# Low parts of weights by accumulating transfers, pair sums in place, the residual through SP's queue

## The chip, the cores and the metric

The kernel runs on one core of a Trainium2 chip. The core has five engines with an instruction queue each: PE (matmul), DVE (vector), ACT (scalar, activations), POOL (GpSimd) and SP (issues transfers). They run beside each other and wait for each other by semaphores; each works through its own queue in order. SBUF is the on-chip memory, PSUM the banks into which PE writes. The metric is the device time of one execution in microseconds (us), lower is better; the median over runs is compared.

## The reference, cut to what matters

One layer on 512 prompt tokens and 32 sample tokens (T = 544), width 1024, FFN width 2816, in float32:

```python
x = x + 0.5 * swiglu(rms_norm(x, ffn1_norm), ffn1_gate, ffn1_up, ffn1_down)
z = rms_norm(x, mix_norm) @ w_in                     # 3584 columns: qa ka va qb fb ib gb
x = x + concat(attention(qa, ka, va), silu(gb) * norm(hgrn2(qb, fb, ib))) @ w_out
x = x + 0.5 * swiglu(rms_norm(x, ffn2_norm), ffn2_gate, ffn2_up, ffn2_down)
def swiglu(x, w_gate, w_up, w_down):
    return (silu(x @ w_gate) * (x @ w_up)) @ w_down
```

The attention is block sparse on the prompt and, on the sample tokens, reads keys and values of 8 sequences from a paged cache. hgrn2 is a gated linear recurrence.

## The kernel before

**Matmuls in two parts.** All activations lie transposed: 128 features on the partitions, 544 tokens along a row, in two halves of 272. A float32 product is made of three faster ones: each operand is split into a high part, rounded (`hi`, float32r), and a low part, the rest (`lo` = value - hi), and `products` issues hi x hi, hi x lo and lo x hi. Of a weight, ACT makes the high part (a cast, `whi<-raw`) and DVE the low part (a subtraction, `wlo<-raw,whi`).

**Weights.** `weight_jobs` lists them in the order of use. A tile of 128 output columns is loaded in two halves ("units") of 4 x 128 rows by SP's queue into a raw buffer (`w_load`), split into a pair whi, wlo (`w_split`, `split_unit`), and freed when PE is done with it (`free_w`), which pumps the next ones (`w_pump`). There are 4 raw buffers and 4 pairs, and at most AHEAD = 4 units are split ahead. In the FFNs further buffers come from the tiles `xh`, `xl` of the normalised input once that is no longer needed (`more_slots`).

**Stages.** FFN1 (about 0 to 400 us of the trace), the middle stage (to about 830) and FFN2 (to the end). In each FFN gate and up of the first NREG = 5 blocks of 128 columns are plain products ("plain blocks"). The other 17 blocks use a scheme of seven products in place of eight (`hidden_paired`, `paired_gemm`): gate and up halves are combined into sums (tiles `S0` to `S3`, in `w_split`), two on DVE and two on POOL, and the right side into differences (`right_factors`, tiles `xw`). `right_factors` is a side task that is stepped between matmuls while the plain blocks run, PACE = 0.8 us after one another; the paired blocks start when it is done. In the middle stage `project` makes the 28 tiles of w_in, between which attention and recurrence run as side tasks; the 8 tiles of w_out follow, which add to the residual `y`. The residual has been parked in DRAM (`xs`) and is loaded back by POOL's queue.

**Order.** A recording layer (`Order`) plans the program by a model of the engines: it gives every instruction a start time and then issues each engine's instructions sorted by those times. So a change of what an operation is modelled to cost, or of which engine does it, moves other instructions too, on all engines. Side tasks fill PE's time as they become ready.

**Names.** `kn`, `qh`, `ql`, `kt`, `y_qk`, `pT`, `sc` belong to the prompt's attention; `KV`, `PT` to the sample's (gathers by POOL from the cache); `rec`, `at`, `oS`, `y_h`, `hkt` to the recurrence; `ob`, `AS`, `attn` to the sample's attention output. In the order printed below numbers behind a name count buffers; `L284` and `L288` are one helper line that records every operation.

Of the kernel before, what the change touches and what calls it, by code (L numbers as in the profile page):

```python
# [30 lines left out]
FGROUPS = ((0, 8), (8, 8), (16, 6))  # L31
# [22 lines left out]
PACE = 0.8  # L54
# [124 lines left out]
class Engine:  # L179
# [74 lines left out]
class Order:  # L254
# [103 lines left out]
    def dma(self, part, size, names, cost=0.06):  # L358
        s = self.fit(part, self.start(part, names), cost)
        e = self.fit("dma", s + cost + 1.5, size / 330e3) + size / 330e3  # L360
# [51 lines left out]

class Build:
# [34 lines left out]

    def weight_jobs(self):
# [7 lines left out]
        def plain(m, nk, r0, c0):  # L457
            out.append({"paired": False, "src": quarters(m, nk, r0, c0), "nk": nk // 2, "raw": [], "done": 0})

        def ffn(p):  # L460
            gate, up, down = (a[p + n][0] for n in ("_gate", "_up", "_down"))
            for g0, ng in FGROUPS:
                for f in range(g0, g0 + ng):
                    if f < NREG:
                        plain(gate, KD, 0, 128 * f)
                        plain(up, KD, 0, 128 * f)
                    else:
                        out.append({"paired": True, "nk": KD // 2, "raw": [], "done": 0,
                                    "src": quarters(gate, KD, 0, 128 * f) + quarters(up, KD, 0, 128 * f)})
                for m in range(KD):  # L470
                    plain(down, ng, g0, 128 * m)

        ffn("ffn1")
        for n, j in IN_ORDER:
            plain(a["w_in"][0], KD, 0, COLS[n] + 128 * j)
        for m in range(KD):
            plain(a["w_out"][0], KD, 0, 128 * m)
        ffn("ffn2")
        return out

    def room(self, kind, job):

        free = [x for x in self.slots[kind] if x["used"] < x["bufs"] and (x["extra"] is None or job["paired"])]
# [13 lines left out]
    def more_slots(self, pool):  # L497

        for i in range(KD):
            if i < 2:  # L500
                for t in ("xh", "xl"):
                    self.slots["raw"].append({"pool": pool, "tags": (f"{t}{i}",), "bufs": 1, "used": 0, "freed": [],
                                              "extra": pool})
            else:
                self.slots["w"].append({"pool": pool, "tags": (f"xh{i}", f"xl{i}"), "bufs": 1, "used": 0,
                                        "freed": [], "extra": pool})
# [9 lines left out]
    def w_load(self):  # L516
# [7 lines left out]
        self.nc.sync.dma_start(raw[:, :job["nk"]], job["src"][len(job["raw"])])  # L524
# [5 lines left out]
    def split_unit(self, src, nk, x):  # L530
        nc = self.nc
        hi, lo = self.take_slot(x, (F32R, F32R))
        nc.scalar.copy(hi[:, :nk], src[:, :nk])
        nc.vector.tensor_tensor(lo[:, :nk], src[:, :nk], hi[:, :nk].bitcast(F32), op=ALU.subtract)
        return hi, lo, x

    def w_split(self):
# [4 lines left out]
        if len(job["raw"]) <= (3 if job["paired"] else n):  # L542
            return False
        x = self.room("w", job)
        if x is None:
            return False
        nk = job["nk"]
        if job["paired"]:
            (a11, a12, a21, a22) = (r for r, _ in job["raw"])
            if n == 0:  # L550
                S = [self.tl(self.sums, [128, 4, 128], f"S{i}") for i in range(4)]
                for i, (e, p, q, op) in enumerate(((self.nc.vector, a21, a22, ALU.add),
                                                   (self.nc.vector, S[0], a11, ALU.subtract),
                                                   (self.nc.gpsimd, a11, a21, ALU.subtract),
                                                   (self.nc.gpsimd, a12, S[1], ALU.subtract))):
                    e.tensor_tensor(S[i][:, :nk], p[:, :nk], q[:, :nk], op=op)
                job["units"] = (a11, S[1], S[0], a12, S[2], S[3], a22)
            src = job["units"][n]
            self.units.append(self.split_unit(src, nk, x))
            drop = {0: (0, 2), 3: (1,), 6: (3,)}.get(n, ())  # L560
        else:
            self.units.append(self.split_unit(job["raw"][n][0], nk, x))
# [9 lines left out]
    def w_pump(self):  # L572
        while (len(self.units) < AHEAD and self.w_split()) or self.w_load():
# [69 lines left out]
    PAIRED = ((0, 0, True), (1, 4, True), (2, 3, True), (0, 1, False), (1, 5, False), (2, 2, False), (1, 6, False))  # L643

    def paired_gemm(self, xw, nk, evacs):
# [6 lines left out]
        for (b, r, first), evac in zip(self.PAIRED, evacs):  # L652
            w, = self.next_w(1)
            for k in range(nk):
                xh, xl = xw[k]
                self.products(ps[b], w, k, xh[:, r], xl[:, r], first and k == 0, k == nk - 1, not first)
# [4 lines left out]
    def right_factors(self, pool, x, gain):  # L661


# [4 lines left out]

        def lows(hi, lo, r, src):
            nc.scalar.copy(hi[:, r], src)  # L670
            nc.vector.tensor_tensor(lo[:, r], src, hi[:, r].bitcast(F32), op=ALU.subtract)

        def diff(out, p, q):
            nc.vector.tensor_tensor(out, p, q, op=ALU.subtract)

        for k in range(n):

            home, th, tl = self.hidden_home
# [1166 lines left out]
```

## Time and profile before

| | |
|---|---|
| median of 3 runs | 1205.38 us (1205.19 to 1206.52) |
| the profiled execution | 1210.65 us, its span 1208.9 us |
| mean granted clock of PE | 0.99 |
| DMA traffic | 144.74 MB, mean 120 GB/s |
| q1, transfers issued by SP and ACT | 106.60 MB, 30.6% of 16 engines' time |
| q0, transfers issued by POOL | 36.32 MB, 9.1% |

The profile is of one execution, and its times are counted from the span's start. PE's busy time says little alone, since matmuls overlap: a matmul of 272 columns is shown with some 0.29 us, but the next one starts 0.125 us later. The pace, the idle time and its releaser ("<-DVE kn" behind a row: PE had waited for DVE's write of kn) tell more. The granted clock falls to half for some microseconds around stretches in which PE stands still.

### The profile page before, as it was taken

What the parts mean: (1) busy time and instruction counts of PE and PEld (TensorE: products, weight loads), DVE (VectorE), ACT (ScalarE), POOL (GpSimd) and SP (SyncE); (2) the same over time, 40 slices, a digit from 0 to 9 for tenths busy, and PEclk for the clock granted to TensorE, in tenths of its full rate; (3) what the DMA queues carried; (4) which work ended last, traced back from release to release, by engine and by line L of the source; (5) the groups of instructions that cost most, each with busy time, mean ns of one, the idle gap of its engine ahead of it and who ended that gap; (6) DMA issues with size and microseconds to landing.
All of it is one profiled execution on the core that took longest, in us unless ns stands there. A gap on an engine that the chain in (4) does not pass through costs nothing.

```text
span 1208.9 us, 26320 instructions
## 1 busy us (share of the span) xinstructions
PE 1178.1 (97%) x10571; PEld 1113.7 (92%) x10571; DVE 858.5 (71%) x1729; ACT 551.9 (46%) x1125; POOL 228.3 (19%) x211
## 2 busy tenths in 40 slices
PE   8999999999999999989999999899999999999998
PEld 8989999999999988878878867799999999999998
DVE  6988559954875698877776557667977488736843
ACT  6455246532654345554556433344554266524632
POOL 3012012200202401000332344220020023102200
PEclk9999999999999999989999999899999999999999
DMA  5244453333314642322565776352344323323222
GB/s 161 79 123 114 133 148 97 97 106 87 87 54 135 193 129 69 97 72 74 181 195 160 235 262 222 111 158 79 93 118 131 97 81 104 106 87 88 63 79 82
DMA packets 216238, 144.74 MB, mean 120 GB/s; under 512 B 12035, under 2 KB 204067, under 8 KB 216116
## 3 DMA queue, kind: packets, MB, share of 16 engines
q1 hardware_dynamic: 205588, 106.60, 30.6%
q0 software_dynamic: 10432, 36.32, 9.1%
q8 instruction: 83, 1.36, 0.5%
q14 instruction: 39, 0.32, 0.1%
q10 hardware_dynamic: 96, 0.14, 0.0%
HBM read 133.94 MB, written 11.83 MB: 121 GB/s over the span
## 4 chain that ended last, share of the span: by engine, by line
PE 77%; DVE 13%; ACT 3%; DMA 3%; issue 2%; SPq 1%; POOL 0%; DVEq 0%; ACTq 0%; POOLq 0%
PE mm L284 51%; PE sm L284 26%; DVE wlo L284 3%; DVE xl L284 2%; DVE xwl L284 1%; DMA raw<-ffn_down 1%; ACT xh L284 1%; DVE t_h L284 1%; SPq L284 1%; ACT whi L284 1%; DVE hl L284 1%; ACT sq L284 1%; DMA raw<-ffn_up 1%; DVE S L284 1%; DMA KV<-cache_v,idx 1%
## 5 line engine op out<-in xcount | busy, mean ns | idle before, releaser
L284 PE MATMUL mm<-xh,whi 128*128 128x272 f32 x1216 | 365.0, 300 | 1.0 <-DVE t_g L284 0.5
L284 PE MATMUL mm<-xl,whi 128*128 128x272 f32 x1216 | 352.4, 290 | 5.4 <-DVE xl L284 5.2
L284 PE MATMUL mm<-xh,wlo 128*128 128x272 f32 x1216 | 353.2, 290 | 1.1 <-DVE wlo L284 1.1
L284 ACT CAST whi<-raw 128x512 fp32r<-128x512 f32 (+1 forms) x230 | 138.7, 604 | 261.4 <-PE mm L284 192.3
L284 PEld LDWEIGHTS mm<-xh,whi 128*128 128x128 f32 x1216 | 231.5, 190 | 18.2 <-issue 15.7
L284 PEld LDWEIGHTS mm<-xl,whi 128*128 128x128 f32 x1216 | 231.3, 190 | 6.4 <-DVE xl L284 6.2
L284 PEld LDWEIGHTS mm<-xh,wlo 128*128 128x128 f32 x1216 | 231.0, 190 | 2.1 <-DVE wlo L284 2.1
L284 DVE TENSOR_TENSOR wlo<-raw,whi 128x512 fp32r<-128x512 f32 (+1 forms) x230 | 165.1, 727 | 81.0 <-ACT whi L284 77.4
L284 POOL TENSOR_TENSOR S<-raw,raw 128x512 f32<-128x512 f32 x18 | 30.4, 1691 | 380.9 <-DMA raw<-ffn_up 261.1
L284 PE MATMUL mm<-hh,whi 128*128 128x272 f32 x352 | 101.5, 288 | 0.3 <-DVE x L284 0.3
L284 PE MATMUL mm<-hh,wlo 128*128 128x272 f32 x352 | 101.1, 287 | 0.0
L284 PE MATMUL mm<-hl,whi 128*128 128x272 f32 x352 | 101.1, 287 | 0.0
L284 PE MATMUL mm<-xwh,xh 128*128 128x272 f32 x296 | 85.4, 288 | 1.3 <-DVE t_h L284 0.8
L284 PE MATMUL sm<-xwl,xh 128*128 128x272 f32 x296 | 85.3, 288 | 0.0
L284 PE MATMUL mm<-xwl,xh 128*128 128x272 f32 x296 | 85.3, 288 | 0.0
L284 PE MATMUL sm<-xwh,xh 128*128 128x272 f32 x296 | 85.2, 288 | 0.0
L284 PE MATMUL mm<-xwh,xl 128*128 128x272 f32 x296 | 85.2, 288 | 0.0
L284 PE MATMUL sm<-xwh,xl 128*128 128x272 f32 x296 | 85.2, 288 | 0.0
L284 DVE TENSOR_TENSOR xl<-S,xh 128x512 fp32r<-128x512 f32 x84 | 66.0, 796 | 4.1 <-ACT xh L284 3.7
L284 PEld LDWEIGHTS mm<-hh,whi 128*128 128x128 f32 x352 | 66.3, 188 | 0.7 <-ACT whi L284 0.5
L284 ACT CAST xh<-S 128x512 fp32r<-128x512 f32 x84 | 51.8, 620 | 32.7 <-DVE S L284 13.7
L284 PEld LDWEIGHTS mm<-hh,wlo 128*128 128x128 f32 x352 | 66.2, 188 | 0.0
(325 smaller groups left out, 2639.2 us busy)
## 6 DMA issues: line engine op xcount, KB each, us to landing
raw<-ffn_down SPq DMA_DIRECT2D x64, 256.0 KB
raw<-ffn_gate SPq DMA_DIRECT2D x56, 256.0 KB
raw<-ffn_up SPq DMA_DIRECT2D x56, 256.0 KB
raw<-w_in SPq DMA_DIRECT2D x56, 256.0 KB
raw<-ffn_down SPq DMA_DIRECT2D x32, 192.0 KB
xl<-ffn_gate SPq DMA_DIRECT2D x16, 256.0 KB
xh<-ffn_up SPq DMA_DIRECT2D x16, 256.0 KB
xl<-ffn_up SPq DMA_DIRECT2D x16, 256.0 KB
```

The source lines that it names most:

```text
L284: call(*map(real, args), **{k: real(v) for k, v in kw.items()})
```

## The change

1. The low part of every unit of w_in and w_out (56 and 16), and of the second unit of gate and up in the FFNs' plain blocks (18), is made without DVE: ACT writes -hi into wlo, and a transfer issued by POOL adds the raw weight to it (`transfer` in `split_unit`). The raw buffer is held until that transfer has landed. There are six whi, wlo pairs in place of four, and in the middle stage up to six units are split ahead (AHEAD_MIX).
2. A paired block's sums are made in place, with other signs: a21 + a22 by an accumulating transfer (POOL's queue), a11 - a21 becomes a11 + a21 on POOL, and two in-place sums on DVE. The tiles S0 to S3 are gone; the extra buffers are ten raw ones and three pairs (were four and six). The first unit needs one raw half loaded, not four. The last one's parts are made with the second's. Right factors follow these signs (`Factors`), two steps each 1.1 us.
3. The residual `y` is loaded through SP's queue.
4. Smaller: the first up product is read from PSUM without copies, the first projection runs its two halves of tokens interleaved, POOL's ring for transfer descriptors gets 8192 bytes of a partition, and the planner has costs for transfers issued by POOL. The code for a paired down product (`down_paired`, FGROUPS[True]) is there, but both FFNs are called without it.

```diff
-PACE = 0.8
+AHEAD_MIX = 6
+PACE = 1.1
...
             if op == "dma_start":
-                s = self.order.dma(self.part, 4 * args[1].shape[0] * self.free(args[1]), names)
+                pool = self.part == "pool"
+                s = self.order.dma(self.part, 4 * args[1].shape[0] * self.free(args[1]), names,
+                                   1.3 if pool else 0.06, 3.0 if "accum_op" in kw else 1.5)
...
+class Factors:
...
+    def first(self):
+        return self.one(0, 0) + [self.diff(0, 1, 0)] + self.one(1, 0)
+    def right(self):
+        nc = self.nc
+        return [lambda: nc.vector.scalar_tensor_tensor(self.raw(0), self.raw(3), -1.0, self.raw(0),
+                                                       op0=ALU.mult, op1=ALU.subtract),
+                lambda: nc.vector.tensor_tensor(self.raw(1), self.raw(1), self.raw(3), op=ALU.add)] + self.two(2, 0)
+    def left(self):
+        return self.two(4, 2) + [self.diff(2, 2, 0)] + self.one(6, 2)
...
+        def paired(kind, nk, a11, a12, a21, a22, transfer):
+            job(kind, [a11, a21, a21 if transfer else None, a22, a12], nk)
+            out[-1]["transfer"] = transfer
...
         raw, = self.take_slot(x, (F32,))
-        self.nc.sync.dma_start(raw[:, :job["nk"]], job["src"][len(job["raw"])])
+        raw_k = raw[:, :job["nk"]]
+        i = len(job["raw"])
+        if job["paired"]:
+            parts = [r[:, :job["nk"]] for r, _ in job["raw"]]
+        if job["src"][i] is None:
+            self.nc.gpsimd.tensor_tensor(raw_k, parts[0], parts[1], op=ALU.add)
+        else:
+            self.nc.sync.dma_start(raw_k, job["src"][i])
...
+        if job["paired"] and i == 3:
+            self.nc.gpsimd.dma_start(parts[1], raw_k, accum_op=ALU.add)
...
-    def split_unit(self, src, nk, x):
+    def split_unit(self, src, nk, x, transfer=False):
+
         nc = self.nc
         hi, lo = self.take_slot(x, (F32R, F32R))
         nc.scalar.copy(hi[:, :nk], src[:, :nk])
+        if transfer:
+            nc.scalar.activation(lo[:, :nk], src[:, :nk], AF.Identity, scale=-1.0)
+            nc.gpsimd.dma_start(lo[:, :nk], src[:, :nk], accum_op=ALU.add)
+            return hi, lo, x
         nc.vector.tensor_tensor(lo[:, :nk], src[:, :nk], hi[:, :nk].bitcast(F32), op=ALU.subtract)
...
+            a11, s1, s3, a22, a12 = ([r for r, _ in job["raw"]] + [None] * 5)[:5]
+            if n in (1, 5):
+
+                out, p = (a11, s1) if n == 1 else (a12, a11)
+                self.nc.vector.tensor_tensor(out[:, :nk], out[:, :nk], p[:, :nk], op=ALU.add)
+            src = (a11, a11, s1, a12, s3, a12, a22)[n]
...
-            self.units.append(self.split_unit(job["raw"][n][0], nk, x))
+            self.units.append(self.split_unit(job["raw"][n][0], nk, xs[0], job["mixer"] or n == 1 and job["start"]))
...
-    PAIRED = ((0, 0, True), (1, 4, True), (2, 3, True), (0, 1, False), (1, 5, False), (2, 2, False), (1, 6, False))
+    PAIRED = ((0, 0, True), (1, 2, True), (2, 1, True), (0, 4, False), (1, 3, False), (2, 5, False), (1, 6, False))
...
-                      "w": [{"pool": self.wp, "tags": ("whi", "wlo"), "bufs": 4, "used": 0, "freed": [], "extra": None}]}
+                      "w": [{"pool": self.wp, "tags": ("whi", "wlo"), "bufs": 6, "used": 0, "freed": [], "extra": None}]}
...
-        yield from self.gemm(self.xg, KD, evac)
+        yield from self.gemm(self.xg, KD, evac, both=self.z_used == 1)
...
-                nc.gpsimd.dma_start(x[k], xspill[k])
+                nc.sync.dma_start(x[k], xspill[k])
...
-    nc = bacc.Bacc("TRN2", target_bir_lowering=False, num_devices=1)
+    nc = bacc.Bacc("TRN2", target_bir_lowering=False, num_devices=1, dynamic_dma_scratch_size=8192)
```

What this does to the order is shown at three places. The first is DVE in the prompt's third pair of heads, behind the scaling of kt by y_qk; before:

```order
L284 TENSOR_TENSOR z_6991<-mm_6822,R_5311 128x272
L284 TENSOR_TENSOR z_6991<-mm_6925,R_5311 128x272
L284 TENSOR_TENSOR wlo_7005<-raw_6742,whi_6954 128x512
L284 TENSOR_TENSOR wlo_7016<-raw_6751,whi_6977 128x512
L284 SCALAR_TENSOR_TENSOR kn_1288_7010<-sm_6997,qkg,kn_1288_7010 64x512
L284 TENSOR_TENSOR ql_7027<-qn_6937,qh_1289_6994 64x512
L284 SCALAR_TENSOR_TENSOR kn_1290_7025<-sm_6997,qkg,kn_1290_7025 64x512
```

and with the change, from behind the same scaling:

```order
L288 COPY pT_1237_6986<-sm_6929 128x512
L288 TENSOR_TENSOR z_6994<-mm_6857,R_5320 128x272
L288 TENSOR_TENSOR ql_7006<-qn_6932,qh_1247_6988 64x512
L288 TENSOR_SCALAR KS<-sm_7017,qkg 128x32
L288 TENSOR_TENSOR QB<-qn_6932,sm_7019 64x8x4 x2
L288 SCALAR_TENSOR_TENSOR kn_1246_7022<-sm_7011,qkg,kn_1246_7022 64x512
L288 SCALAR_TENSOR_TENSOR kn_1248_7034<-sm_7011,qkg,kn_1248_7034 64x512
```

The two low parts ahead of kn are gone, and one ql, KS and QB now stand ahead of it. On PE, between the two transposes of y_qk and the first product of kn with qh, there stood 6 matmuls of 272 columns and 5 transposes of z; now there are 30 and 5.

The second place is DVE where w_out begins (`rec` are the recurrence's outputs, `xl` the low parts of w_out's input); before, with the last small steps on y_h and the scaling of at and oS ahead (a low part wlo of the kernel's old form stands nine rows further up):

```order
L284 SCALAR_TENSOR_TENSOR t_h_10425<-t_h_10425,v_h_10395 128x6
L284 SCALAR_TENSOR_TENSOR y_h_10400<-t_h_10425,y_h_10400 128x6
L284 TENSOR_TENSOR at_10353<-at_10353,y_h_10400 128x512
L284 TENSOR_TENSOR oS_10342<-oS_10342,y_h_10400 128x256
L284 SCALAR_TENSOR_TENSOR ob_10129<-sm_10371,sst_9826,ob_10129 128x128
L284 TENSOR_TENSOR xl_1918_10444<-rec_6409,xh_1917_10429 128x544
L284 TENSOR_TENSOR hkt_10446<-hvts_10250,fc 96x512
L284 TENSOR_TENSOR xl_1920_10456<-rec_8232,xh_1919_10449 128x544
```

and with the change:

```order
L288 SCALAR_TENSOR_TENSOR rec_10345<-rec_10345,z_10228 128x544
L288 TENSOR_TENSOR xl_1879_10396<-rec_6408,xh_1878_10386 128x544
L288 TENSOR_TENSOR xl_1881_10411<-rec_8251,xh_1880_10407 128x544
L288 SCALAR_TENSOR_TENSOR ob_10181<-sm_10348,sst_9877,ob_10181 128x128
L288 TENSOR_SCALAR v_h_10468<-ms_10427 128x6
```

The low parts of rec come first now. On PE the first products of w_out move in between the last products with KV, and the transposition of ob stands right ahead of w_out's products with attn, where 12 matmuls of 272 columns and seven other products stood between.

The third is POOL where the sample's gathers of values run; with the change:

```order
L288 DMA KV_1679_9310<-cache_k,idx_1821 128x1024
L288 DMA KV_1685_9347<-cache_v,idx_1821 128x1024
L288 DMA wlo_1687_9360<-raw_1646_9183 128x512
L288 DMA wlo_1689_9382<-raw_1647_9193 128x512
L288 DMA KV_1697_9409<-cache_v,idx_1821 128x1024
```

Before, only gathers and the recurrence's sums stood there; the transfers into wlo have moved in between.

More of the change, by code (lines that the diff above doesn't have):

```diff
@@ L455, in quarters, with turns, job @@
                     for r in (r0, r0 + h)]
-        def plain(m, nk, r0, c0):
-            out.append({"paired": False, "src": quarters(m, nk, r0, c0), "nk": nk // 2, "raw": [], "done": 0})
-        def ffn(p):
+        def turns(m, nk, r0, c0):
+            rows = m[128 * r0:128 * (r0 + nk), c0:c0 + 128].rearrange("(k two p) m -> two p k m", two=2, p=128)
+            return [rows[0], rows[1]]
+        def job(kind, src, nk):
+            out.append({"kind": kind, "src": src, "nk": nk // 2, "raw": [], "done": 0, "paired": kind is not None, "mixer": False})
@@ L463, in ffn @@
                 for f in range(g0, g0 + ng):
                     if f < NREG:
-                        plain(gate, KD, 0, 128 * f)
-                        plain(up, KD, 0, 128 * f)
-                    else:
[L468 to L473, printed above, removed]
+                        plain(gate, KD, 0, 128 * f, start=True)
@@ new lines, in ffn @@
+                        plain(up, KD, 0, 128 * f, start=True)
+                    else:
+                        paired("a", KD, *quarters(gate, KD, 0, 128 * f), *quarters(up, KD, 0, 128 * f), pairs)
+                for m in range(0, KD, 2):
+                    if pairs:
+                        paired("a", ng, *turns(down, ng, g0, 128 * m), *turns(down, ng, g0, 128 * (m + 1)), True)
+                    else:
+                        plain(down, ng, g0, 128 * m)
+                        plain(down, ng, g0, 128 * (m + 1))
@@ L769, in have_R, with raw_hidden, split, go @@
         return self.R is not None
+    def raw_hidden(self, i, hs):
+        if not self.pairs:
+            pool, name = self.hidden_raw
+            u = self.tl(pool, [128, T], name, bufs=2)
+            hs.append([self.tl(self.hidden_home(2 * i + k)[0], [128, T], self.hidden_home(2 * i + k)[1], F32R)
+                       for k in range(2)])
+            hi, lo = hs[i]
+            def split():
+                self.nc.scalar.copy(hi, u)
+                self.nc.vector.tensor_tensor(lo, u, hi.bitcast(F32), op=ALU.subtract)
+            return u[:, self.cols(0)], u[:, self.cols(1)], split, lambda: None
+        p, odd = divmod(i, 2)
+        if not odd:
+            hs.append(Factors(self, lambda k: self.hidden_home(7 * p + k), [(self.sums, "U0"), (self.sums, "U1")]))
+        f = hs[p]
+        def go(steps):
+            for s in steps:
+                s()
+        if odd:
+            return f.raw(2), f.raw(3), lambda: go(f.left()), lambda: go(f.right())
+        return f.raw(0), f.raw(1), lambda: go(f.first()), lambda: None
     def hidden(self, pool, i, hs):
@@ L884, in setup @@
         self.gains = self.cp.tile([128, 3, KD], F32, name="gains")
+        self.ngains = self.cp.tile([128, 3, KD], F32, name="ngains")
     def small(self, rp):
@@ L1046, in load_x @@
         ps = [[self.mm(), self.mm()], [self.sm(), self.sm()]]
-        out = [self.tl(pool, [128, T], t, bufs=2) for t in ("t_s", "t_h")]
+        out = self.tl(pool, [128, T], "t_s", bufs=2)
         LAG = 3
```

231 lines of the change are left out of this document (137 added, 94 removed).

## The prediction

> **What bounds the kernel.** I read the page first, then busy time by stage, then PE's waits, then PE and DVE in order of time at the two longest of those waits.
>
> ```profile
> PE 1178.1 (97%) x10571; PEld 1113.7 (92%) x10571; DVE 858.5 (71%) x1729; ACT 551.9 (46%) x1125; POOL 228.3 (19%) x211
> 40.00:80.00 40.00, 38.53 (x296) 37.15 (x295) 38.13 (x74) 18.64 (x33) 1.10 (x1) 1.00 0.29 75
> 80.00:120.00 40.00, 38.40 (x300) 37.52 (x300) 34.30 (x53) 24.49 (x50) 9.74 (x8) 1.00 0.50 139
> 120.00:400.00 280.00, 279.68 (x2218) 277.15 (x2217) 192.74 (x328) 126.60 (x242) 46.40 (x32) 1.00 0.36 106
> 440.00:520.00 80.00, 78.37 (x598) 67.98 (x597) 67.42 (x181) 42.30 (x107) 6.58 (x7) 0.98 0.30 87
> 520.00:560.00 40.00, 36.81 (x257) 31.43 (x257) 32.43 (x81) 19.46 (x45) 1.77 (x1) 0.87 0.28 80
> 700.00:760.00 60.00, 57.09 (x972) 42.41 (x973) 39.72 (x109) 17.54 (x50) 29.27 (x30) 1.00 0.74 248
> 760.00:780.00 20.00, 14.51 (x163) 12.46 (x161) 13.47 (x37) 7.20 (x21) 0.51 (x1) 0.83 0.25 81
> 920.00:1200.00 280.00, 280.00 (x2241) 279.91 (x2240) 180.06 (x309) 119.61 (x231) 42.70 (x27) 1.00 0.31 91
> ```
>
> The first row is the whole span. In the others the columns are the stretch, its length, then busy time of PE, weight load, DVE, ACT and POOL, the granted PE clock, the DMA engines' share and GB/s. From 120 to 400 us and from 920 to 1200 us (the FFN blocks) PE has no idle time worth the name: 279.68 and 280.00 of 280. PE's work is the same before and after, so nothing can be won there. What can be won lies in FFN1's first blocks (40 to 120) and in the middle stage, where PE idles and in two stretches also runs at a lower clock (0.87, 0.83). In 440 to 560 DVE is busy 67.42 + 32.43 of 120 us, and 38.13 of 40 in 40 to 80.
>
> ```profile
> PE mm L284 <- DVE xl L284: 5.2, 3, 3.1
> PE sm L284 <- DVE kn L284: 4.1, 3, 3.2
> PE sm L284 <- DMA KV<-cache_v,idx: 1.7, 2, 1.0
> 526.05 0.29 PE L284 MATMUL mm<-xl,whi 128*128 128x272 f32 x1
> 526.18 0.29 PE L284 MATMUL mm<-xh,wlo 128*128 128x272 f32 x1
> 533.02 0.55 PE L284 MATMUL sm<-kn,qh 128*128 128x256 f32 x1 [3.19 <-DVE kn L284]
> 540.86 0.43 PE L284 MATMUL mm<-xl,whi 128*128 128x272 f32 x1
> 541.08 0.43 PE L284 MATMUL mm<-xh,wlo 128*128 128x272 f32 x1
> 541.91 0.29 PE L284 MATMUL mm<-xl,whi 128*128 128x272 f32 x1
> 769.53 0.59 PE L284 MATMUL mm<-xl,whi 128*128 128x272 f32 x1 [3.10 <-DVE xl L284]
> 774.03 0.29 PE L284 MATMUL mm<-xh,whi 128*128 128x272 f32 x1
> 776.29 0.39 PE L284 MATMUL mm<-xl,whi 128*128 128x272 f32 x1 [1.22 <-DVE xl L284]
> ```
>
> Matmuls overlap, so their pace is read from start to start. Before the wait at 533 it is 0.13 us (526.05, 526.18); behind it 0.22 (540.86, 541.08), until full pace returns at 541.9. So the 3.19 us wait is followed by 8.9 us at about half pace, which lose another 4.4. The 3.10 us wait at 769.53 is followed by 4.5 us at half pace, which lose 2.2, and a 1.22 us wait. **These two places cost 3.2 + 4.4 = 7.6 and 3.1 + 2.2 + 1.2 = 6.5 us**, and both wait for DVE.
>
> ```profile
> 527.95 2.65 DVE L284 TENSOR_TENSOR wlo<-raw,whi 128x512 fp32r<-128x512 f32 x2
> 530.62 0.74 DVE L284 SCALAR_TENSOR_TENSOR kn<-sm,qkg,kn 64x512 fp32r<-64x512 f32 x1
> 531.40 0.68 DVE L284 TENSOR_TENSOR ql<-qn,qh 64x512 fp32r<-64x512 f32 x1
> 532.12 0.75 DVE L284 SCALAR_TENSOR_TENSOR kn<-sm,qkg,kn 64x512 fp32r<-64x512 f32 x1
> 528.28 1.77 POOL L284 TENSOR_TENSOR kt<-kt,gkrow 128x640 f32<-128x640 f32 x1 [32.41 <-PE sm L284]
> ```
>
> At the first place two weight subtractions stand on DVE right ahead of the kn that PE waits for, and take 2.65 us, while POOL's kt sum runs.
>
> **The change, part by part.** Sums are made against the profiled execution: 1210.65 us, a span of 1208.9 with 1.75 around it. The median of the runs shown, 1205.38, lies 5.27 below, so the result is moved down by 5.27.
>
> ```profile
> L284 DVE TENSOR_TENSOR wlo<-raw,whi 128x512 fp32r<-128x512 f32 (+1 forms) x230 | 165.1, 727 | 81.0 <-ACT whi L284 77.4
> L284 ACT CAST whi<-raw 128x512 fp32r<-128x512 f32 (+1 forms) x230 | 138.7, 604 | 261.4 <-PE mm L284 192.3 <-issue 42.4 <-PE sm L284 5.3
> L284 POOL DMA_DIRECT2D y<-xs x8 | 4.4, 580 | 22.2 <-PE mm L284 22.2
> L284 POOL DMA_INDIRECT KV<-cache_v,idx x32 | 31.5, 984 | 43.5 <-PE sm L284 40.0 <-issue 1.2 <-PE mm L284 0.8
> 702.71 6.53 DMA KV<-cache_v,idx
> 888.19 4.18 DMA raw<-ffn_up
> ```
>
> *Low parts in the middle stage* (72 units: 56 of w_in, 16 of w_out). DVE loses 72 x 0.727 = 52.3 us, ACT gains 72 x 0.604 = 43.5 (the negated copy, priced as the cast of the same size), POOL 72 issues at 0.58 (a plain load) to 0.98 (a gather), 42 to 71 us. ACT was busy 42.30 + 19.46 of 120 us in 440 to 560, so its share hides there. What counts is the two places.
>
> Place 1: the order puts no subtraction ahead of kn, and moves 24 more matmuls of 272 columns, 24 x 0.125 = 3.0 us of PE work, between the transposes of y_qk and the first product with kn. DVE's chain there is hardly shorter, since a pT copy and the other kn remain and POOL's kt sum may now hold up ql, but PE's cover grows by about what it waited. I take the whole **-7.6** (bounds 0 and -7.6).
>
> Place 2: the three xl of rec now stand ahead of the small steps on y_h and at; the 6.5 us go. Next late is the chain behind the matmul on ob, with no other work on PE:
>
> ```profile
> 770.83 0.41 PE L284 MATMUL sm<-fc,ob 128*128 128x128 f32 x1
> 771.28 0.46 DVE L284 COPY AS<-sm 64x64 f32<-64x64 f32 x2 [0.57 <-PE sm L284]
> 772.41 0.17 DVE L284 COPY attn<-AS 128x32 f32<-128x32 f32 x1
> 772.62 0.65 ACT L284 CAST xh<-attn 128x544 fp32r<-128x544 f32 x1 [6.05 <-DVE attn L284]
> 775.52 0.71 DVE L284 TENSOR_TENSOR xl<-attn,xh 128x544 fp32r<-128x544 f32 x1
> ```
>
> It takes 0.41 + 0.46 + 0.17 + 0.65 + 0.71 = 2.4 us. Net **-4** (bounds -6.5, and +1 if that wait also brings half pace).
>
> *Latency of a low part.* It now arrives by a transfer. For the duration the nearest rows are a 512 KB gather on the same queue (6.53 us behind others) and a 256 KB load (4.18): I take 4 to 5. It is hidden: with six w pairs a tile's units are split two tiles ahead, 2 x 48 x 0.125 = 12 us, where it was one. The cost if the cover fails is the first rival. In 700 to 760 some ten added transfers share queue and engines (share 0.74) with the gathers, for which PE waited 1.7 us in all: **+1** (bounds 0 and +4).
>
> *FFN plain blocks*: 18 transfers, 13.1 us off DVE, of which 8 lie in FFN1 from 30 to 88 us. PE's idle time in 40 to 120 is 1.47 + 1.60; the right factors keep DVE as busy as before, their paced steps end in front of the last gate's product. **-1** (0 to -3.1).
>
> *Pair sums in place*: of four sums of a block (two on DVE, two on POOL) DVE keeps two, POOL one, and one becomes a transfer. In 120 to 400 and 920 to 1200 PE's saturation hides all of it. At the first block of each FFN the second unit waits for a load, then a transfer, then the sum; behind that sum DVE holds two low parts and the product t_h. Against this the first unit now needs one load instead of four. **+0.5** for both (bounds -2, +6: about 3 each). The signs turned in it are subtractions and scales in place of the same operations: nothing.
>
> *Residual through SP*: takes 4.4 us off POOL and puts eight loads in front of the last two w_out halves on SP's queue, then FFN2's; units are four ahead there. 0 (bounds 0, +2). Reading the first up product from PSUM, the halved ring for POOL's descriptors, the first projection's interleaved halves: 0; the ring has no row, and could at most hold POOL for one landing, 6.5 us, which PE need not see.
>
> *The rest of the middle stage* gains from a less loaded DVE: -1. A new order also makes waits of its own; for one of the kind seen, without half pace, I add **+2**. Sum: -7.6 - 4 + 1 - 1 + 0.5 - 1 + 2 = -10.1.
>
> **The rivals.** (1) *Slower: the transfers pace w_out.* A raw buffer is now held through load (4.18), two ACT copies (1.2), issue (0.6 to 1.0) and landing. With four buffers and a unit used every 3.0 us (half a tile's 6.0) it must turn in 12 us, so this begins when landing takes over 6 us. At 13 us (twice the gather) the loop is 19, each unit is (19 - 12)/4 = 1.8 us late, some 10 units of w_out behind the six split ahead lose 18: 1210.65 - 10 + 18 - 5.27 = 1213. It outweighs the gain from about 10 us of landing on. For: one queue with the gathers, and an accumulation has to read both sides; against: half a gather's bytes. The Trainium skill (DMA: Bandwidth & Descriptors, section on the anatomy of one DMA on the SWDGE path) fits such transfers as 2.0 us plus bytes over 436e3; for 256 KB that would be an estimate of 2.6 us and no wait at all, but it was fitted to plain loads, and no row of this trace shows an accumulating one.
>
> (2) *Same: the stalls only move.* The two places are gone, others of that size come up in an order laid out anew, or ACT's added copies are late in place of DVE's: 1203 to 1207. For: the two waits named are 3.2 and 4.3 of the 30.8 us (1208.9 - 1178.1) in which PE is idle; most of the rest is in waits of about a microsecond and less, at many places.
>
> (3) *DVE holds up POOL's issues.* If each issue had to wait out what DVE has in hand, 2.65 us by the longest row of DVE above, loop (1) would be 6.2 + 5 + 2.65 = 13.9, 0.5 us late a unit, 5 over ten; with the same delay at the two first paired blocks, 5 more: 1195.3 + 10 = 1205. Against it stands the row that follows.
>
> ```profile
> L284 POOL DMA_INDIRECT KV<-cache_v,idx x32: 932/939/1709, 419.8 to 757.3; - x32
> ```
>
> Issues of 32 gathers beside a busy DVE took 0.94 us at the median and 1.71 at most, 0.77 more. The Trainium skill (SBUF — State Buffer, section on two separate sides) says that an operation of DVE in a two-port mode locks POOL out of writing descriptors, and tells of a 620 ns transfer that took 3100. The row does not bear out a delay of that size.
>
> That the change does not do what it says can be set aside: the order shows no low part of the middle stage left on DVE.
>
> **How the numbers follow.** Forecast: 1210.65 - 10.1 - 5.27 = **1195.3**, chance 0.66 for all outcomes below 1203. Same (2, and 3 in part): 0.15. Slower (1, with 3 at its worst): 0.19. A measurement of this kernel can tell about 0.2% from no change, 2.4 us: faster is below 1203.0, slower above 1207.8. Low end: -7.6 - 6.5 - 3.1 - 2 - 1 = -20.2, 1185. High end: all terms at their worst at once give +1 + 4 + 6 + 2 - 1 + 2 = +14, 1219, past rival (1); cutting off what is least likely I stop at 1209. Some 0.17 stays above it and 0.03 below 1185.
>
> **What would show it.** In the profile after: the group wlo<-raw on DVE falls from 230 to 166 while 90 transfers into wlo appear on POOL; no wait of PE for kn over 1 us and a clock of 1.00 in 520 to 560; at the start of w_out one wait of 2 to 3 us for xl behind ob in place of three; POOL's accumulating transfers landing in 4 to 6 us and no waits of PE for wlo. Waits of PE or of ACT for wlo's transfer or for raw<-w_out between 780 and 830 would show rival (1); waits of PE for DVE of the same total elsewhere in 440 to 760, rival (2); POOL issues of 3 us, rival (3). I am wrong if PE stops where it did not before: at the first paired blocks (near 82 and 890) or in the gathers' stretch.

## The result, and the profile after

The changed kernel took **1219.15 us** (median of 4 runs, 1218.0 to 1224.02) against 1205.89 before (4 runs): a ratio of **1.0118**, 95% interval 1.0089 to 1.0146. That is 24 us above the forecast of 1195.3 and above the range's upper end of 1209. The profiled execution took 1219.56 us, with a span of 1217.8.

Where the time went is seen best by PE's own progress. PE issues the same 7656 products of 272 columns in both kernels. The table gives the start of the last of each so many fortieths of them, worked out from the trace's starts (us). The profile of before was taken on an execution of 1210.65 us, 4.8 above its median, so a lead or lag of a few us against it is rough:

| fortieth | what ends there | before | after | difference | change since the row above |
|---|---|---|---|---|---|
| 16 | FFN1, start of w_in | 414.1 | 413.6 | -0.4 | -0.4 |
| 23 | w_out, first two tiles | 786.4 | 777.7 | -8.6 | -8.2 |
| 24 | w_out, third to sixth tile | 810.4 | 813.3 | +2.9 | **+11.5** |
| 27 | FFN2's plain blocks | 886.0 | 887.8 | +1.8 | -1.1 |
| 28 | FFN2's first two paired blocks | 909.9 | 920.5 | +10.6 | **+8.8** |
| 40 | end | 1203.2 | 1212.5 | +9.3 | -1.3 |

So the middle stage did gain some 8 us. It was given back, and more, at two places: right after w_out begins, and in FFN2's first paired block. The first row is the whole span of the changed kernel, the others its stretches (length, then busy time of PE, weight load, DVE, ACT and POOL, the granted clock, DMA share, GB/s):

```profile
PE 1180.5 (97%) x10571; PEld 1117.7 (92%) x10571; DVE 780.5 (64%) x1662; ACT 600.8 (49%) x1223; POOL 281.8 (23%) x293
40.00:80.00 40.00, 40.00 (x322) 40.00 (x321) 37.06 (x78) 22.63 (x42) 6.17 (x6) 1.00 0.53 120
80.00:120.00 40.00, 36.95 (x277) 35.97 (x276) 32.10 (x52) 22.10 (x45) 8.91 (x8) 0.96 0.72 183
440.00:480.00 40.00, 37.53 (x289) 31.65 (x288) 30.17 (x91) 27.25 (x72) 6.72 (x7) 0.91 0.52 126
520.00:560.00 40.00, 39.31 (x310) 33.85 (x307) 27.29 (x75) 23.82 (x56) 7.77 (x9) 1.00 0.54 126
780.00:800.00 20.00, 10.85 (x70) 10.63 (x69) 5.08 (x10) 6.07 (x10) 4.70 (x6) 0.74 0.67 187
790.00:795.00 5.00, 4.58 (x20) 4.58 (x21) 3.24 (x7) 2.59 (x4) 0.44 (x1) 0.50 0.90 301
880.00:920.00 40.00, 36.08 (x251) 35.17 (x251) 25.54 (x41) 17.89 (x36) 7.35 (x7) 0.87 0.60 151
```

and of the kernel before, for two of these stretches:

```profile
780.00:800.00 20.00, 20.00 (x159) 20.00 (x160) 11.34 (x20) 9.78 (x16) 7.16 (x10) 1.00 0.63 194
880.00:920.00 40.00, 38.73 (x309) 38.51 (x308) 33.20 (x52) 22.74 (x47) 9.45 (x7) 1.00 0.43 124
```

DVE lost the work it was meant to lose (858.5 to 780.5 us). In 520 to 560 PE was busy 36.81 us at a clock of 0.87; now it is 39.31 at 1.00. But from 780 to 800 PE, which had no idle time there before, is busy 10.85 of 20 us. Four of PE's longest waits, and SP's for the transfers into wlo, summed over the span (us in total, times, longest):

```profile
PE mm L288 <- DVE y L288: 9.2, 1, 9.2
PE sm L288 <- ACT sq L288: 3.0, 1, 3.0
PE sm L288 <- DVE kt L288: 2.8, 2, 2.5
PE mm L288 <- ACT sq L288: 2.1, 1, 2.1
SPq L288 <- DMA wlo<-raw: 318.5, 83, 34.8
```

The waits for kn of before are gone, and those for xl fell from 5.2 to 1.9 us on these products; in their place stands one wait of 9.2 us for y, the residual. Now the queues and engines around it in order of time, first of the changed kernel:

```profile
775.11 0.99 POOL L288 DMA_DIRECT2D wlo<-raw  x1 [19.22 <-ACT wlo L288]
779.35 1.73 POOL L288 DMA_DIRECT2D wlo<-raw  x2 [1.85 <-ACT whi L288]
778.50 7.08 SPq L288 DMA_DIRECT2D raw<-w_out  x4
785.87 4.25 SPq L288 DMA_DIRECT2D y<-xs  x8
789.93 0.79 DVE L288 TENSOR_TENSOR y<-mm,y 128x272 f32<-128x272 f32 x2 [18.83 <-DMA y<-xs]
790.42 0.60 PE L288 MATMUL mm<-xh,whi 128*128 128x272 f32 x1 [9.15 <-DVE y L288]
```

and of the kernel before:

```profile
782.70 4.39 POOL L284 DMA_DIRECT2D y<-xs  x8 [22.20 <-PE mm L284]
783.66 19.52 SPq L284 DMA_DIRECT2D raw<-w_out  x8
788.43 0.79 DVE L284 TENSOR_TENSOR y<-mm,y 128x272 f32<-128x272 f32 x2 [0.23 <-DMA y<-xs]
```

Before, y went through POOL's queue, which held nothing else, and arrived 0.23 us after DVE was ready for it: DVE had no reserve there, though PE did not wait. Now y's loads stand on SP's queue *behind* four loads of w_out. The first of those goes at 778.50, 3.4 us after the transfer into wlo of 775.11, because its raw buffer is free only when that transfer has landed. The last two go at 783.31 and 785.22, right behind the landings (783.26 and 785.15 in the trace) of the two transfers issued from 779.35 on. So y leaves at 785.87. Without the sum into y the PSUM buffers of w_out's first tiles stay taken, PE cannot begin the second half of the third tile at 781, and behind the wait it runs at a clock of 0.50 (790 to 795). The sum into y begins only 1.5 us later than before (789.93 and 788.43); but PE gets there 8.5 us sooner, and the stop takes back what the middle stage had gained.

In FFN2's first paired block (ACT, then SP, then PE):

```profile
892.59 0.62 ACT L288 CAST whi<-raw 128x512 fp32r<-128x512 f32 x1 [2.81 <-DMA raw<-ffn_gate]
897.54 0.62 ACT L288 CAST whi<-raw 128x512 fp32r<-128x512 f32 x1 [4.05 <-DMA raw<-ffn_gate]
888.15 0.44 SPq L288 DMA_DIRECT2D raw<-ffn_gate  x1
891.87 1.81 SPq L288 DMA_DIRECT2D raw<-ffn_gate  x1
898.50 0.82 PE L288 MATMUL sm<-xw,xh 128*128 128x272 f32 x2 [2.99 <-ACT sq L288]
```

ACT's casts wait for loads that were issued only at 888.15 and 891.87; ACT's copy of PSUM (sq), for which PE waits, stands behind the second of these casts. A block with sums in place keeps a11, a21, s and a22 in the four raw buffers, and a12 is loaded only when a22 has been split.

The third stop lies where w_in begins; at the 17th fortieth the changed kernel is 5.3 us behind. First a window of the changed kernel, then the same of the one before (the DMA engines' share is 1.05 where it was 0.68), then the chain in the changed kernel:

```profile
404.00:420.00 16.00, 15.19 (x122) 14.97 (x121) 5.68 (x19) 5.47 (x11) 6.89 (x11) 1.00 1.05 227
404.00:420.00 16.00, 15.20 (x123) 14.98 (x122) 8.21 (x23) 4.46 (x9) 9.89 (x18) 1.00 0.68 192
439.99 0.62 ACT L288 CAST whi<-raw 128x512 fp32r<-128x512 f32 x1 [3.04 <-DMA raw<-w_in]
441.65 1.01 DVE L288 TENSOR_REDUCE ms_qk<-sq 128x8 f32<-128x512 f32 x2 [2.46 <-ACT sq L288]
447.19 1.30 PE L288 MATMUL sm<-fc,kt 128*128 128x128 f32 x5 [2.47 <-DVE kt L288]
```

A cast on ACT waits 3.04 us for a late load of w_in; the squares of the k norm stand behind it on ACT, and so DVE and PE wait in turn.

### The profile page after: what moved, and what is told of

The parts are those of the page before. It is cut to its first block, busy times and chain, and to the rows that moved or that the text cites. A ratio compares the mean times of both kernels' runs of the same rounds, so it can differ in the third digit from the quotient of the medians.

```text
span 1217.8 us, 26505 instructions
## 1 busy us (share of the span) xinstructions
PE 1180.5 (97%) x10571; PEld 1117.7 (92%) x10571; DVE 780.5 (64%) x1662; ACT 600.8 (49%) x1223; POOL 281.8 (23%) x293
## 4 chain that ended last, share of the span: by engine, by line
PE 85%; DVE 5%; DMA 4%; issue 3%; ACT 1%; POOL 1%; SPq 0%; POOLq 0%; ACTq 0%; DVEq 0%
PE mm L288 58%; PE sm L288 27%; DMA wlo<-raw 1%; DMA raw<-ffn_gate 1%; DMA raw<-w_in 1%; DMA SC<-rsample 0%; DMA xin<-x_prompt 0%; DVE ms_qk L288 0%; DVE wlo L288 0%; DVE xl L288 0%; SPq L288 0%; POOL wlo L288 0%; DVE t_qk L288 0%; ACT sq L288 0%; POOL KV L288 0%
## 5 line engine op out<-in xcount | busy, mean ns | idle before, releaser
L288 PE MATMUL mm<-hw,whi 128*128 128x272 f32 x704 | 132.3, 288 | 0.0
L288 POOL DMA_DIRECT2D wlo<-raw x90 | 81.3, 931 | 218.2 <-ACT wlo L288 181.8
L288 PE MATMUL sm<-xw,whi 128*128 128x272 f32 x648 | 124.3, 290 | 0.4 <-ACT t_g L288 0.4
L288 PE MATMUL mm<-xw,whi 128*128 128x272 f32 x648 | 123.2, 288 | 0.8 <-ACT t_g L288 0.8
L288 PEld LDWEIGHTS mm<-hw,whi 128*128 128x128 f32 x704 | 110.2, 188 | 0.2 <-issue 0.2
L288 PEld LDWEIGHTS sm<-xw,whi 128*128 128x128 f32 x648 | 102.8, 190 | 0.6 <-ACT t_g L288 0.6
L288 PEld LDWEIGHTS mm<-xw,whi 128*128 128x128 f32 x648 | 101.9, 189 | 1.0 <-ACT t_g L288 1.0
L288 PE MATMUL mm<-hw,wlo 128*128 128x272 f32 x352 | 101.2, 287 | 0.0
L288 PE MATMUL sm<-xw,wlo 128*128 128x272 f32 x324 | 94.0, 290 | 0.0
L288 PE MATMUL mm<-xw,wlo 128*128 128x272 f32 x324 | 93.3, 288 | 0.0
```

What stands on the lines that cost most here:

```text
L288: call(*map(real, args), **{k: real(v) for k, v in kw.items()})
```

## The experiments

Thirteen kernels were run, each in five rounds beside the kernel before on the same chip: the first four of the table on one chip, the others on another, where the changed kernel was run again. The totals below are the ratios to before with their intervals; a single profiled execution can lie some us off its median, so the profiles are used for places and not for totals. The middle columns give PE's lead or lag in us against the profile of before, at the fortieths of the first table. Inside the middle stage other work is ordered differently from kernel to kernel, so there a single fortieth tells where time went rather than exactly how much:

| kernel | ratio (95%) | 16 | 23 | 24 | 27 | 28 | 40 |
|---|---|---|---|---|---|---|---|
| y_pool | 1.0081 (1.0057 to 1.0105) | 0.1 | -5.1 | 5.2 | 4.0 | 11.0 | 9.9 |
| mix_dve | 1.0034 (1.0017 to 1.0050) | -0.3 | -4.3 | 1.9 | 0.7 | 7.8 | 6.6 |
| paired_raw2 | 1.0060 (1.0041 to 1.0078) | -0.1 | -7.0 | 4.0 | 2.9 | 6.9 | 5.6 |
| raw6_small_ring | 1.0078 (1.0054 to 1.0103) | 0.2 | -3.2 | 7.7 | 6.6 | 10.6 | 9.3 |
| changed_again | 1.0103 (1.0086 to 1.0121) | 1.5 | -8.4 | 2.5 | 1.3 | 10.3 | 9.1 |
| outdve_ypool | 1.0027 (1.0013 to 1.0040) | 0.9 | -9.1 | -9.1 | -10.3 | -1.1 | -2.4 |
| pairs_own | 1.0002 (0.9986 to 1.0019) | -3.0 | -11.3 | -0.3 | -1.5 | -1.4 | -2.4 |
| pairs_own_outdve_ypool | 0.9927 (0.9912 to 0.9942) | -2.7 | -7.5 | -7.5 | -8.8 | -8.7 | -9.5 |
| best_win_dve | 0.9923 (0.9902 to 0.9944) | -3.4 | -6.0 | -6.0 | -7.3 | -6.7 | -7.4 |
| best_raw5 | 0.9888 (0.9866 to 0.9909) | -4.1 | -16.6 | -16.6 | -17.9 | -17.8 | -19.1 |
| best_nostart | 1.0007 (0.9988 to 1.0025) | 2.3 | -6.4 | -6.4 | -7.7 | -6.8 | -6.5 |
| raw5_win_dve | 0.9918 (0.9905 to 0.9931) | -4.1 | -6.1 | -6.1 | -7.4 | -7.3 | -8.5 |
| paired_raw2_pooladd | 1.0063 (1.0046 to 1.0079) | 3.5 | -1.3 | 9.1 | 8.0 | 9.8 | 10.3 |

**y_pool**: the residual through POOL again.

```diff
-                nc.sync.dma_start(x[k], xspill[k])
+                nc.gpsimd.dma_start(x[k], xspill[k])
```

> The changed kernel with one part undone: the eight loads of the residual y go through POOL's queue again. Theory A (a queue that stands still): in the changed kernel y's loads stand on SP's queue behind four loads of w_out, which wait for raw buffers that the transfers into wlo still hold; PE's 9.2 us wait for DVE y at 781 is that queue. On POOL the loads can go as soon as the last four transfers into wlo are issued (781.1 instead of 785.9), so the wait shrinks by about 4 to 5 us and the time by 4 to 8 us, to 1211 to 1215; the stops at 444, 86 and 895 us stay. Rival A' (y cannot be loaded earlier, because the memory under it comes free late): the wait stays at 9 us and the time within 2 us of 1219.

Some 0.2 to 0.4% below the changed kernel (1.0103 and 1.0118), with intervals that overlap, and less than theory A had for the wait itself. POOL and DVE there:

```profile
784.19 4.22 POOL L288 DMA_DIRECT2D y<-xs  x7
792.23 0.79 DVE L288 TENSOR_TENSOR y<-mm,y 128x272 f32<-128x272 f32 x2 [17.80 <-DMA y<-xs]
```

y's loads go right behind w_out's last transfers on POOL, as theory A says, but DVE gets the first only 8.0 us later. Two transfers stand ahead of them on POOL and four loads of w_out go beside them; which of the two it is that delays y, this run does not show. PE still waits 7.9 us. Rival A' seemed right about the size; whether A or A' held, the next ones had to tell.

**mix_dve**: low parts of the middle stage on DVE, y on SP.

```diff
-... job["mixer"] or n == 1 and job["start"]))
+... n == 1 and job["start"]))
```

> The changed kernel with the low parts of the middle stage's 72 units computed by DVE again (subtraction), y still loaded through SP. Theory B (the transfers hold the raw buffers until they land, and so keep SP's queue standing): w_out's wait for y shrinks to under 3 us and the wait for kt at 444 goes, since a buffer is free about 1 us after its cast; the waits for DVE at 500 to 780 come back in part; 1208 to 1214. The 8 us at FFN2's first paired block stay. Rival B' (the transfers cost nothing, only the queue chosen for y does): w_out's wait stays at 7 us or more and the time gets longer than 1219 because DVE has its 52 us back.

The wait for y falls to 3.4 us, a little above the 3 of theory B, and the stop at 444 us is gone (at the 17th fortieth the kernel is 1.8 us ahead of before, the changed one 5.3 behind). B' is out. The time, 1.0034 of before, would be 1210 us beside the 1205.89 of the first table, inside theory B's band.

**paired_raw2**: two more raw buffers for paired blocks.

```diff
         self.pairs, self.sums, self.hidden_raw = pairs, wide, (pool, "t_h")
+        self.more_slots("a", pool, [f"r{i}" for i in range(2)], [])
```

> The changed kernel with two more raw buffers for paired blocks alone, open from the start of each FFN (4 + 2 before the first paired block instead of 4). Theory C (the sums in place need a fifth buffer in a block: a11, a21, s, a22 fill the four, and a12 is loaded only when a22's low part is done): the stops at 86 and 895 us (2.4 and 3.3 us of waiting and about 10 us of half clock behind the second) go, 7 to 12 us faster, 1207 to 1212. Rival C' (the accumulating transfer between the second and third loads is what is late): the stops stay, since the transfer is as before; within 2 us of 1219.

From the 27th to the 28th fortieth PE takes 27.9 us, against 32.7 in the changed kernel and 23.9 before: the buffers cure 4.8 of the 8.8 us there. In FFN1 nothing is won in the end. The ratio of 1.0060 is some 5 to 7 us below the changed kernel, where theory C had 7 to 12; C', which had no gain, is out. What is left was seen in this order (POOL, DVE, PE):

```profile
891.38 0.88 POOL L288 DMA_DIRECT2D raw<-xh  x1 [3.24 <-DMA xh<-ffn_up]
898.11 0.69 DVE L288 TENSOR_TENSOR raw<-raw,raw 128x512 f32<-128x512 f32 x1 [1.98 <-DMA raw<-xh]
900.88 0.52 PE L288 MATMUL sm<-xw,whi 128*128 128x272 f32 x2 [2.14 <-DVE t_h L288]
```

The accumulating transfer issued at 891.38 ends DVE's wait only at 898.11, beside some ten loads.

**raw6_small_ring**: six raw buffers everywhere.

```diff
-... "tags": ("raw",), "bufs": 4 ...
+... "tags": ("raw",), "bufs": 6 ...
-... dynamic_dma_scratch_size=8192)
+... dynamic_dma_scratch_size=4096)
```

> The changed kernel with six raw buffers instead of four everywhere (the ring for POOL's descriptors is 4096 instead of 8192 bytes, to make room). If theories B and C hold (buffers held until a transfer lands are the bound at 444, 781, 86 and 895 us), all four stops shrink: 15 to 22 us faster, 1197 to 1204. If only C holds: 1207 to 1212. If the ring matters, POOL's issues of transfers take over 1.5 us at the median instead of 0.9, and the time is longer.

1.0078 is far from the 15 to 22 us expected. The wait for y stays (9.1 us): more buffers do not move y to the front of a queue. The paired block falls to 27.9 us, as with two more. At w_in's start the wait for kt goes, but other stops stand in its place. The smaller ring does not show: POOL's issues into wlo take 0.87 us at the median in both kernels.

**changed_again, outdve_ypool**: the changed kernel on the second chip, and w_out's low parts on DVE with y on POOL. Without the mark `True` w_out's units are also split at most four ahead, not six; the same goes for w_in's where that mark is taken off below.

```diff
-            plain(a["w_out"][0], KD, 0, 128 * m, True)
+            plain(a["w_out"][0], KD, 0, 128 * m)
-                nc.sync.dma_start(x[k], xspill[k])
+                nc.gpsimd.dma_start(x[k], xspill[k])
```

> The changed kernel as it is, on this chip, to compare the three below and the four of the first call with it. All theories: 1.010 to 1.014 of the kernel before, with the 9 us wait for y at 781 and the two stops in the first paired blocks.

It gives 1.0103, with a wait of 8.4 us for y.

> The changed kernel with w_out's 16 low parts by DVE again and y through POOL; w_in's 56 low parts and the FFN's 18 stay transfers. Theory D (at the start of w_out the change has filled both queues that y could take: SP with loads that wait for raw buffers, POOL with transfers that wait for ACT): with POOL empty y's loads go when the last xl of rec is read (about 772), 5 us and more before the third tile's first half ends, and the 9 us wait and the half clock behind it go: 8 to 12 us below the changed kernel. Rival D' (the memory under y is what comes late, as the wait of 7.9 us that stayed with POOL alone would let one think): the wait stays at 5 us or more.

```profile
773.63 4.37 POOL L288 DMA_DIRECT2D y<-xs  x8 [21.83 <-PE mm L288]
```

With nothing ahead of it on POOL, y goes at 773.63 and the stop at the third tile is gone. The 23rd to 24th fortieth costs as much as before the change (lead of 9.1 us at both ends), and the ratio falls from 1.0103 to 1.0027, 9.2 us. Theory D holds, D' is out: the memory under y was free in time, both queues were taken.

**pairs_own**: pair sums in four tiles again.

```diff
-            job(kind, [a11, a21, a21 if transfer else None, a22, a12], nk)
+            job(kind, [a11, a12, a21, a22], nk)
...
+                S = [self.tl(self.sums, [128, 4, 128], f"S{i}") for i in range(4)]
+                for i, (e, p, q) in enumerate(((self.nc.vector, a21, a22), (self.nc.vector, S[0], a11),
+                                               (self.nc.gpsimd, a11, a21), (self.nc.gpsimd, a12, S[1]))):
+                    e.tensor_tensor(S[i][:, :nk], p[:, :nk], q[:, :nk], op=ALU.add)
```

(with four raw and six w slots more in the paired blocks, as before the change)

> The changed kernel with the pair sums in four tiles of their own again, two sums on DVE and two on POOL, four loads a block, no accumulating transfers there. Theory C in full (the sums in place need more buffers, loads and steps one behind another in a block): the 32.7 us from the 27th to the 28th fortieth of PE's products go back to the 23.9 of before; about 8 us below the changed kernel, FFN1 unchanged within 1 us. Rival C'' (half of it comes from the paced right factors or from the two steps a turn): the stretch keeps 27 us or more, as with two more raw buffers (27.9).

1.0002 against 1.0103: **12.2 us** (1.01% of 1207.6). The 27th to 28th fortieth takes 23.9 us, as before the change, and FFN1, which the expectation left as it was within 1 us, wins 2.6 to 4.5 us at the 16th (3.0 ahead, where the two profiles of the changed kernel are 0.4 ahead and 1.5 behind). Theory C holds in full, C'' is out; FFN1's part was missed.

**pairs_own_outdve_ypool**: both.

> Both edits together: of the change there stay w_in's and the FFN's low parts by transfers, six w pairs, the new factors and the ring. If the losses add up as theories C and D say, 16 to 20 us below the changed kernel, which is 2 to 6 us below the kernel before (ratio 0.995 to 0.998). If w_in's transfers themselves cost time (their stop at 444 us, 5 us late at the 17th fortieth), not below the kernel before.

0.9927, 1.7% below the changed kernel (21 us), more than the 16 to 20 expected: the two losses add up (9.2 and 12.2), and what is left of the change gains 8.8 us (0.73% of 1207.6).

**best_win_dve, best_raw5, best_nostart**: three edits of that kernel.

```diff
-            plain(a["w_in"][0], KD, 0, COLS[n] + 128 * j, True)
+            plain(a["w_in"][0], KD, 0, COLS[n] + 128 * j)
```

> The last kernel of the second call (pair sums in tiles of their own, w_out's low parts on DVE, y through POOL) with w_in's 56 low parts on DVE too, split as far ahead as in the kernel before: no transfer is left in the middle stage. Theory E (the transfers of w_in's low parts bring the gain of the middle stage): the wait for kn with its half clock and the waits for DVE at 440 to 640 come back, 7 to 9 us slower than that kernel, ratio to before 0.999 to 1.003. Rival E' (the gain comes from the new factors and the steps of the FFN, or from a new order as such): ratio stays below 0.996.

Theory E falls. The wait for kn is back at 529 us, as it said, and from the 18th to the 19th fortieth PE takes 58.2 us where the kernel with transfers takes 43.3. But the other stretches are faster, from the start of w_in on (29.4 us instead of 35.7 from the 16th to the 17th), and the time is the same. With four raw buffers w_in's transfers gain nothing.

```diff
-... "tags": ("raw",), "bufs": 4 ...
+... "tags": ("raw",), "bufs": 5 ...
-... dynamic_dma_scratch_size=8192)
+... dynamic_dma_scratch_size=4096)
```

> The same kernel (0.9927 of before) with five raw buffers instead of four (POOL's ring 4096 bytes). Theory F (with transfers a raw buffer is held too long, so w_in's loads come late, ACT waits for them and what stands behind on ACT, the squares of the k norm, reaches PE late at 442 us): that 3 us wait shrinks to under 1 us, 2 to 4 us faster, ratio 0.989 to 0.991. Rival F' (the loads are late because the 16 DMA engines are full, share 0.96 to 1.05 between 404 and 436 us): the wait stays, within 2 us.

Theory F holds: the wait for kt falls from 2.7 to 0.3 us. The first line is a window of it, the others are PE's longest waits:

```profile
420.00:436.00 16.00, 14.89 (x304) 13.44 (x303) 14.83 (x41) 6.32 (x12) 12.12 (x17) 1.00 1.02 268
PE mm L288 <- DVE xl L288: 3.4, 3, 2.2
PE sm L288 <- DMA KV<-cache_v,idx: 2.6, 4, 1.0
```

From 420 to 436 us the DMA engines are as full (1.02), and the wait that F' would have left is gone. At 0.9888 this is the fastest kernel of the study, 13.5 us below the one before on its chip (1193.89 against 1207.37).

```diff
-... job["mixer"] or n == 1 and job["start"]))
+... job["mixer"]))
```

> The same kernel (0.9927 of before) with the low parts of the FFN's 18 second plain units on DVE again. The prediction's term: these transfers bring 1 us (0 to 3.1), in FFN1 between 30 and 88 us, so 0 to 3 us slower, ratio 0.993 to 0.995. Rival: DVE has room there without them, and the transfers only take a raw buffer longer; same time or faster.

1.0007 instead of 0.9927, 9.7 us and more than the 0 to 3 expected; the rival is out. In the profiles 4.6 us of it are lost by the fourth fortieth (3.3 behind instead of 1.3 ahead), in FFN1, where PE's wait for the first paired block's wlo grows from 2.3 to 3.8 us. Where the rest lies the one profile, 2.8 us longer, does not show.

**raw5_win_dve**: the fastest kernel with w_in's low parts on DVE.

> The kernel with five raw buffers (0.9888 of before), w_in's low parts on DVE instead of transfers: no transfer is left in the middle stage. Theory G (the fifth buffer is what w_in's transfers lacked, and only with it do they pay): the wait for kn near 529 us and its half clock come back, 4 to 7 us slower, ratio 0.992 to 0.995. Rival G' (the fifth buffer helps by itself, whoever makes the low parts): ratio 0.987 to 0.990.

```profile
PE sm L288 <- DVE kn L288: 3.7, 2, 3.2
520.00:560.00 40.00, 36.80 (x260) 32.11 (x259) 32.30 (x77) 18.07 (x42) 1.77 (x1) 0.91 0.29 82
```

The wait for kn and the lower clock are back. 0.9918 lies just under the band of theory G and above that of G'. The fifth buffer alone changes nothing (0.9923 without it); with it w_in's transfers, together with six units split ahead instead of four, are worth about 0.3%, 3.6 us, though the two intervals just overlap.

**paired_raw2_pooladd**: in paired_raw2, the accumulating transfer as an addition on POOL.

```diff
-            self.nc.gpsimd.dma_start(parts[1], raw_k, accum_op=ALU.add)
+            self.nc.gpsimd.tensor_tensor(parts[1], parts[1], raw_k, op=ALU.add)
```

> The changed kernel with two more raw buffers for paired blocks (0.6% over before in the first call), and the accumulating transfer a21 += a22 of a block replaced by an addition on POOL in place. Theory H (of the 8.8 us lost at FFN2's first paired block, the part that the buffers do not cure is the transfer's landing: in that run it was issued at 891.4, and the sum behind it started at 898.1): the stretch from the 27th to the 28th fortieth falls from 27.9 to 24 to 25.5 us, 3 us faster than with the buffers alone, ratio about 1.003 to 1.004. Rival H' (the sums stand one behind another whoever adds): stays at 27 us or more.

The 27th to 28th fortieth takes 25.7 us (27.9 with the transfer), about what theory H said; H' is out for that place. The time is no better, 1.0063, where H had 1.003 to 1.004: FFN1 lies 3.5 us behind, and while POOL adds, DVE's operations beside it get longer:

```profile
898.89 1.79 DVE L288 TENSOR_TENSOR raw<-raw,r 128x512 f32<-128x512 f32 x1
900.21 1.63 POOL L288 TENSOR_TENSOR xl<-xl,xl 128x512 f32<-128x512 f32 x1
```

## Why the prediction was wrong

**Residual through SP: this step failed.** It was put at 0 (bounds 0 and +2) because it looked at what y's loads stand *in front of*. It did not ask what they stand *behind*: four loads of w_out that wait for raw buffers. The text had the numbers for it, since rival (1) has the loop in which a raw buffer is held by load, copies, issue and landing; it applied it only to the units' own pace. Measured: +11.5 us from the 23rd to the 24th fortieth, a 9.15 us wait and the half clock behind it. The queue chosen for y is not enough to explain it: with w_out's transfers and y on POOL PE waits 7.9 us, with y on SP but no transfers in the middle stage 3.4, and only with both undone is the stop gone (outdve_ypool, 9.2 us faster). So the term that was put at nothing is y's way behind work that w_out's transfers hold up, on either queue.

**Pair sums in place: mis-sized, and its cause not seen.** The term was +0.5 with a bound of about 3 us for each first block. Measured: 8.8 us at FFN2's, and 12.2 us in all by the kernel that undoes it. The prediction counted a load, a transfer and a sum one behind another, but not that a block now needs a fifth raw buffer where four are free (4.8 of the 8.8 us), nor that such a transfer ends DVE's wait only 6.7 us after its issue, among some ten loads. A stop near 890 was one of the prediction's own signs of being wrong, and it came. These two terms were forecast at 0.5 together and cost 9.2 and 12.2 by the kernels that undo them, which is 21 of the 24 us that the forecast is off.

**Place 1** was right as a place: no wait for kn, clock 1.00 in 520 to 560. But it was no net gain of w_in's transfers: what they win there they lose at w_in's start with four raw buffers. The sum took the gain from one place and gave the latency of a transfer a cost only where PE waits for a low part; the loads that wait for the buffer had none.

**Place 2** was right about the wait and wrong about the gain. There is one wait of about 2 us behind ob, but the lower clock came with it, which the prediction had only as a bound. The rows are of the changed kernel; before, the clock in 760 to 780 was 0.83 too.

```profile
765.17 0.60 PE L288 MATMUL mm<-xh,whi 128*128 128x272 f32 x1 [1.99 <-ACT xh L288]
760.00:780.00 20.00, 17.17 (x126) 15.69 (x125) 7.75 (x18) 7.63 (x13) 2.52 (x4) 0.83 0.25 58
765.00:770.00 5.00, 4.67 (x19) 4.36 (x20) 2.71 (x7) 2.35 (x5) 0.00 (x0) 0.50 0.15 45
```

From 765.17 to 771.31 PE runs at half pace and loses 2.9 us. With the wait that is 4.9 us where it was 6.5: the place brought some 1.6 us, not 4. That the middle stage as a whole still gained 8.2 us, near the 9.6 of its terms in the sum, is in part luck: best_win_dve is as fast without w_in's transfers.

**Latency.** The transfers into wlo, over the whole changed kernel (issue to landing, us), and POOL's issues of them:

```profile
DMA to landing us min/median/max: 3.1/4.0/7.9
L288 POOL DMA_DIRECT2D wlo<-raw x90 | 81.3, 931 | 218.2 <-ACT wlo L288 181.8 <-PE mm L288 11.4 <-DVE hw L288 7.4
```

4.0 us is the lower end of what the prediction took. The Trainium skill (DMA: Bandwidth & Descriptors, anatomy of one DMA on the SWDGE path) fits a transfer as 2.0 us plus bytes over 436e3, an estimate of 2.6 us for 256 KB. The accumulating ones here took 3.1 at least. Issues of 0.93 us on the mean put rival (3) aside. Rival (1) did not come as it was put, since landing took 4.0 us at the median (7.9 at most) and PE is busy 39.95 of 40 us from 800 to 840; its mechanism, the held buffer, came at another place. PE's waits for the gathers, for which +1 was set, fell from 1.7 to 0.6 us in all.

**FFN plain blocks** bring more than the -1 that was forecast: 4.6 us in FFN1 by the profiles of best_nostart and its parent. In the changed kernel itself the pair sums took that back.

What stays open: what the transfers of w_out are worth where y is out of their way, which was not tried; where most of the 9.7 us of the FFN's transfers lies; and what the other parts left (the new factors, six pairs, the new order) bring.

## What to carry to other kernels

A transfer that is moved to another queue waits for all that stands ahead of it there, so read the waits of those instructions first, and see how much reserve the transfer had where it was (here none: DVE already waited 0.23 us for it). When an engine's operation is replaced by a DMA, its source buffer is held from load to landing; count the buffers on that loop for each stage, and again where a stage starts, before counting the engine time that is saved. Undo the parts one by one: two parts of this change lost 21 us, and without them the rest made the kernel 0.7% faster than before, and 1.1% with one buffer more.

## What the runs showed of the hardware

Eight loads of 272 KB issued on POOL's queue beside four loads of 256 KB and two transfers brought the first to DVE only 8.0 us later (y_pool), where 4.1 us was enough in the changed kernel with y behind the other loads. An addition of two 128x512 tiles on DVE took 0.68 us with POOL idle (the changed kernel at 894.20) and 1.79 while POOL added two tiles (paired_raw2_pooladd at 898.89).

A wait of 9.15 us on PE was followed by a granted clock of 0.50 over the next 5 us, which loses some 2.5 us, while in the kernel before a wait of 3.19 us was followed by 8.9 us at half pace, which lost 4.4. So the loss behind a wait does not follow the wait's length. The clock of the changed kernel was low already while PE still waited:

```profile
785.00:790.00 5.00, 0.00 (x0) 0.00 (x0) 0.07 (x1) 0.00 (x0) 0.00 (x0) 0.50 0.76 238
```

It is 0.50 from 785 to 795, some 10 us, and 0.51 from 531.4 to 541.7 in the kernel before: the low stretch was as long, but half of it fell into the longer wait.
